# Token tiles of the latent q and kv projections on single banks of a PSUM pair

## The chip, the cores and the metric

One core of one Trainium2 chip runs one launch of the whole program. The metric is the device time of that launch in microseconds (us); lower is better. Runs of one kernel are given as the median with the lowest and the highest.

## What is computed

The reference is one inference step of a two-layer decoder for a prompt of 512 tokens and 8 samples of 4 tokens, 544 tokens in all, in float32. The change lies in the first layer's mixer, where multi-head latent attention and an S5 state-space layer stand side by side:

```
def even_mixer(hn, pos, h0_re, h0_im, attend, p):
    proj = hn @ p['w_in']                        # 1024 -> 768 (c_q), 256 (c_kv), 32 (k_r), 512 (u)
    cq = rms_norm(c_q, p['cq_norm'])
    qf = rms_norm((cq @ p['w_uq']).reshape(b, L, MLA_HEADS, MLA_QK), p['q_gain'])
    q = jnp.concatenate([qf[..., :MLA_NOPE], rope(qf[..., MLA_NOPE:], pos)], axis=-1)
    ckv = rms_norm(c_kv, p['ckv_norm'])
    kr = rope(k_r[:, :, None, :], pos)[:, :, 0]
    o_att = attend(q, ckv, kr)                   # keys and values: ckv @ w_ukv
    o_s5, hr, hi = s5_ssm(u, h0_re, h0_im, p)
    out = jnp.concatenate([o_att, o_s5], axis=-1) @ p['w_out']
```

After it come attention over a paged cache, cross-attention to a memory, a squared-ReLU MLP, and a second layer with a gated recurrence. None of that is edited.

## The kernel before

Every float32 matmul is made of three passes over a high and a low part (`mm3`, line 190 is where it issues them): high by high, high by low, low by high.

The first layer's mixer is `even_mixer`. It works in this order of the source: the S5 input `u` (four gemms), the S5 layer in four tiles of eight groups (`s5_layer`), the latent q `cq` (six gemms, line 394 and on), the latent kv `ckv` (loop at line 404), transposes of the kv latents (`plT`, `plTs`), the q heads (loop over two halves of the heads `ch` and five token tiles, lines 464 to 492), and the keys and values `kv` (loop at line 500). The token tiles run in the order 4, 0, 1, 2, 3; tile 4 holds the 32 sample tokens, the others 128 prompt tokens each. A q tile is 18 matmuls (6 blocks of the contraction by 3 passes) of 384 columns, a ckv tile 24 matmuls of 288 columns.

Each tile of S5 is a chain of its own: 16 small DMAs gather the input (`s5U`, line 872, on SP's queue) once the tile before has been read for the last time by its output matmuls; then the matmuls `s5X` (line 898), a scan on VectorE (lines 902 to 915) and the output matmuls `s5Y` (line 942).

The order of instructions on each engine is not written out by hand. A scheduler orders them when the program is built, by a timeline of its own: of what is ready it takes what stands first in the source. On the chip each engine then runs its list strictly in order. Weight loads are given higher priority (`load_w`): they go by SP's queue into a raw buffer (two of them), are split into a high part by ScalarE (line 165) and a low part by VectorE (line 166), in three buffers each. The q weights of one `ch` are three such pieces of two blocks each.

PSUM has eight banks. In this stage `pbig` hands out two tiles of two banks each (tag `big`, two buffers), three more banks are `small` and one is `side`. The q and ckv loops ask for a pair per token tile and use only its first bank:

```
            for t in (4, 0, 1, 2, 3):
                rows = rows_of(t)
                ps = self.pbig(f"q{t}_{ch}")[:, 0, :]
                self.tokmm(ps, (cH, cL), t, wq, 6, 0, 384)
```

A pair can be handed out again when everything that reads it is done. For a q tile that is: squares with sums on ScalarE (line 476), an addition on VectorE (477), a power on GpSimd (478), and four scaled copies on ScalarE (480), the last reader. For a ckv tile it is the scaled write of `lat` on VectorE (414), after the squares (410), an addition (412) and a power (413).

The last q matmul frees the buffers that the kv stage writes: the split `cT` takes the memory of `cH` and `cL`, and the kv weights take that of the q weights. The decode stage's page loads (line 1025, on SP's queue) wait for the last kv matmul.

Of the kernel before, what the change touches and what calls it, by code (L numbers as in the profile page):

```python
# [87 lines left out]
def rows_of(t):  # L88
    return 128 if t < 4 else NSAMP
# [15 lines left out]
class K:  # L105
# [28 lines left out]

    def pbig(self, name):
        return self.ps.tile([128, 2, 512], F32, tag="big", bufs=2, name=name)

    def psm(self, name):
        return self.ps.tile([128, 512], F32, tag="small", bufs=self.nsmall, name=name)
# [177 lines left out]
    def even_mixer(self, gs, beside):  # L317
# [83 lines left out]
        nc.gpsimd.memset(kr[:, 4], 0.0)  # L401
        ssr = IN.tile([128, TT], F32, name="ssr")
        ws = self.load_wk(w, KT, QL, CL + ROPE, "ckv")
        for t in (4, 0, 1, 2, 3):
            rows = rows_of(t)
            ps = self.pbig(f"ckv{t}")[:, 0, :]
            self.tokmm(ps, (H, L), t, ws, KT, 0, CL + ROPE)
            j = self.tp.tile([128, CL], F32, tag="junk", bufs=1, name="junk")
            ssc = self.tp.tile([128, 1], F32, tag="ssc", name="ssc")
            nc.scalar.activation(j[:rows], ps[:rows, :CL], AF.Square, accum_out=ssc[:rows])  # L410
            nc.scalar.activation(kr[:rows, t], ps[:rows, CL:CL + ROPE], AF.Copy, scale=r0[:rows, t:t + 1])
            nc.vector.tensor_scalar(ssc[:rows], ssc[:rows], 1.0 / CL, eq[:rows, t:t + 1], op0=ALU.mult, op1=ALU.add)
            nc.gpsimd.tensor_tensor(out=ssc[:rows], in0=ssc[:rows], in1=self.nhalf[:rows, :1], op=ALU.pow)
            nc.vector.scalar_tensor_tensor(out=self.lat[:rows, t, :CL], in0=ps[:rows, :CL], scalar=ssc[:rows],
                                           in1=gckv[:rows], op0=ALU.mult, op1=ALU.mult)
# [44 lines left out]
        for rows, t in ((128, slice(0, 4)), (NSAMP, slice(4, 5))):  # L460
            nc.vector.scalar_tensor_tensor(out=mq[:rows, t], in0=pst[:rows, t], scalar=QK * EPS / QL, in1=eq[:rows, t],
                                           op0=ALU.mult, op1=ALU.add)
        q_s = k_tok[:NSAMP, 3]
        for ch in range(2):
            wq = self.load_wk(a["w_mla_uq"][0], 6, 384 * ch, 384, f"uq{ch}")
            hs = slice(4 * ch, 4 * ch + 4)
            for t in (4, 0, 1, 2, 3):
                rows = rows_of(t)
                ps = self.pbig(f"q{t}_{ch}")[:, 0, :]
                self.tokmm(ps, (cH, cL), t, wq, 6, 0, 384)  # L470
                q = (q_tok[:, t, hs] if t < 4 else q_s[:, hs])
                p3 = ps[:rows, :384].rearrange("p (h d) -> p h d", h=4)
                sq = self.tp.tile([128, 4, QK], F32, tag="junk", bufs=1, name="qsq")
                ssq = self.tp.tile([128, 4], F32, tag="ssk", name="ssq")
                for i in range(4):
                    nc.scalar.activation(sq[:rows, i], p3[:, i], AF.Square, accum_out=ssq[:rows, i:i + 1])
                nc.vector.tensor_scalar(ssq[:rows], ssq[:rows], mq[:rows, t:t + 1], None, op0=ALU.add)
                nc.gpsimd.tensor_tensor(out=ssq[:rows], in0=ssq[:rows], in1=self.nhalf[:rows, :4], op=ALU.pow)
                for i in range(4):
                    nc.scalar.activation(q[:, i], p3[:, i], AF.Copy, scale=ssq[:rows, i:i + 1])  # L480
                if ch == 0:
                    continue
                q = q_tok[:, t] if t < 4 else q_s
                tmp = self.tp.tile([128, HEADS, ROPE], F32, tag="qrt", bufs=1, name="qrt")
                b = lambda x: x[:rows, t, None, :].to_broadcast([rows, HEADS, x.shape[2]])
                nc.vector.tensor_tensor(out=tmp[:rows, :, :16], in0=q[:, :, NOPE + 16:], in1=b(sin[:, :, :16]),
                                        op=ALU.mult)
                nc.vector.tensor_tensor(out=tmp[:rows, :, 16:], in0=q[:, :, NOPE:NOPE + 16], in1=b(sin[:, :, 16:]),
                                        op=ALU.mult)
                nc.vector.tensor_tensor(out=q[:, :, NOPE:], in0=q[:, :, NOPE:], in1=b(cos), op=ALU.mult)  # L490
                nc.vector.tensor_tensor(out=q[:, :, NOPE:], in0=q[:, :, NOPE:], in1=tmp[:rows], op=ALU.add)
# [7 lines left out]
        for t in (4, 0, 1, 2, 3):  # L499
# [5 lines left out]
            for hf in range(2):  # L505
                ps = pb[:, hf, :]
# [1487 lines left out]
```

## Time and profile before

| | us |
|---|---|
| median of 3 runs (lowest, highest) | 1981.86 (1979.16, 1982.23) |
| the profiled execution | 1982.57 |
| its span, first to last instruction | 1980.8 |
| TensorE busy | 1917.3 (97% of the span) |
| VectorE busy | 1163.0 (59%) |
| ScalarE busy | 804.2 (41%) |
| GpSimd busy | 472.2 (24%) |
| mean granted TensorE clock | 0.986 of full speed |

The profile page has six parts: busy time of each engine, the span in slices, the DMA queues, the chain of work that ended last, the costliest groups of instructions, and the DMA issues. PE is TensorE, PEld its weight loads, DVE is VectorE, ACT is ScalarE, POOL is GpSimd, and SP's queue issues most DMAs. A busy PE is not PE at its peak, since matmuls overlap. The page is an average of stages that differ; the stage in question lies between about 100 and 250 us, so the views of that stretch matter here.

### The profile page before, as it was taken

To read this page: it belongs to the slowest core of one execution; us is meant where nothing else is said; L and a number is where in the kernel's file an instruction comes from. 1 tells how busy PE (TensorE), PEld (TensorE's weight loads), DVE (VectorE), ACT (ScalarE), POOL (GpSimd) and SP (SyncE) were. 2 spreads that over 40 slices of the span, in tenths; PEclk is the share of its full clock that TensorE was granted. 3 is DMA by queue.
4 is the path that set the end of the run, shared out by engine and by line. 5 is a ranking of instruction groups with operands and counts; after the bars stand their busy time and mean duration, and the time that the engine had idled before them with its cause. 6 is when DMAs were issued, how large, how long until landed. Compare 5 with 4: busy or idle time off the path is not lost.

```text
span 1980.8 us, 39933 instructions
## 1 busy us (share of the span) xinstructions
PE 1917.3 (97%) x16089; PEld 1808.6 (91%) x16089; DVE 1163.0 (59%) x2264; ACT 804.2 (41%) x1546; POOL 472.2 (24%) x375
## 2 busy tenths in 40 slices
PE   8888899999999999999999999999999999999998
PEld 7777688889998979999999999999999799999998
DVE  7766566766765557433333568898865563434344
ACT  4455455545554444322222334444444432313131
POOL 4545245656552205000000110111132130000000
PEclk9888999999999999999999999999999999999999
DMA  6221231231334453322322332323325233223222
GB/s 150 71 57 36 59 79 49 54 85 52 93 101 108 145 169 100 96 86 87 95 86 86 91 100 85 101 81 97 91 66 173 85 102 90 86 86 96 86 86 78
DMA packets 317163, 179.42 MB, mean 91 GB/s; under 512 B 52242, under 2 KB 305267, under 8 KB 316979
## 3 DMA queue, kind: packets, MB, share of 16 engines
q1 hardware_dynamic: 289154, 164.47, 28.6%
q10 hardware_dynamic: 26224, 8.06, 1.7%
q0 software_dynamic: 1600, 4.34, 0.8%
q8 instruction: 127, 2.08, 0.4%
q14 instruction: 58, 0.47, 0.1%
HBM read 165.90 MB, written 9.82 MB: 89 GB/s over the span
## 4 chain that ended last, share of the span: by engine, by line
PE 87%; DVE 5%; ACT 2%; issue 2%; SPq 1%; DMA 1%; POOL 1%; ACTq 0%; POOLq 0%; DVEq 0%
PE ps_dn L190 19%; PE ps_up L190 19%; PE kp L1150 9%; PE ps_wo L190 5%; PE ps_hq L190 3%; PE ps_hi L190 3%; PE ps_hf L190 3%; PE ps_hg L190 2%; PE ps_mq L190 2%; PE ps_wmo L190 2%; PE mkv L190 2%; PE s5Y L942 1%; PE ct L289 1%; SPq L1025 1%; PE hatt L1754 1%
## 5 line engine op out<-in xcount | busy, mean ns | idle before, releaser
L190 PE MATMUL ps_dn<-hidH,wH_dn 128*128 128x272 f32 x1024 | 211.4, 287 | 0.0
L190 PE MATMUL ps_dn<-hidH,wL_dn 128*128 128x272 f32 x1024 | 211.2, 288 | 0.0
L190 PE MATMUL ps_up<-actH_f,wH_up 128*128 128x272 f32 x1024 | 211.2, 287 | 0.0
L190 PE MATMUL ps_dn<-hidL,wH_dn 128*128 128x272 f32 x1024 | 210.7, 287 | 0.0
L190 PE MATMUL ps_up<-actH_f,wL_up 128*128 128x272 f32 x1024 | 210.5, 288 | 0.0
L190 PE MATMUL ps_up<-actL_f,wH_up 128*128 128x272 f32 x1024 | 210.4, 287 | 0.0
L1160 POOL TENSOR_TENSOR ss<-ss,nhalf 128x32 f32<-128x32 f32 x32 | 173.7, 5429 | 95.4 <-DVE ss L1158 92.0
L1265 DVE TENSOR_TENSOR h<-ps_dn,h 128x544 f32<-128x544 f32 x64 | 46.4, 725 | 207.2 <-PE ps_dn L190 207.2
L190 PEld LDWEIGHTS ps_dn<-hidL,wH_dn 128*128 128x128 f32 x1024 | 160.2, 188 | 0.0
L190 PEld LDWEIGHTS ps_up<-actL_f,wH_up 128*128 128x128 f32 x1024 | 160.0, 188 | 0.0
L190 PEld LDWEIGHTS ps_dn<-hidH,wL_dn 128*128 128x128 f32 x1024 | 159.6, 189 | 0.1
L190 PEld LDWEIGHTS ps_dn<-hidH,wH_dn 128*128 128x128 f32 x1024 | 159.5, 188 | 0.0
L190 PEld LDWEIGHTS ps_up<-actH_f,wL_up 128*128 128x128 f32 x1024 | 159.4, 188 | 0.0
L190 PEld LDWEIGHTS ps_up<-actH_f,wH_up 128*128 128x128 f32 x1024 | 159.4, 188 | 0.0
L165 ACT ACTIVATE wH_dn<-wraw_dn 128x1024 fp32r<-128x1024 f32 x64 | 68.0, 1063 | 216.6 <-PE ps_dn L190 154.9
L165 ACT ACTIVATE wH_up<-wraw_up 128x1024 fp32r<-128x1024 f32 x64 | 68.0, 1062 | 195.4 <-PE ps_up L190 99.6
L166 DVE TENSOR_TENSOR wL_up<-wraw_up,wH_up 128x1024 fp32r<-128x1024 f32 x64 | 82.8, 1294 | 109.2 <-ACT wH_up L165 107.1
L166 DVE TENSOR_TENSOR wL_dn<-wraw_dn,wH_dn 128x1024 fp32r<-128x1024 f32 x64 | 78.4, 1224 | 67.5 <-ACT wH_dn L165 65.3
L1153 ACT ACTIVATE sq<-kp 128x512 f32<-128x512 f32 x128 | 76.4, 597 | 95.1 <-PE kp L1150 56.9
L253 POOL TENSOR_TENSOR acc_x<-acc_x,sq 128x544 f32<-128x544 f32 x7 | 10.8, 1544 | 349.6 <-issue 327.3
L1155 DVE TENSOR_REDUCE ss<-sq 128x8 f32<-128x512 f32 x128 | 86.8, 678 | 0.0
L165 ACT ACTIVATE hidH<-mu 128x544 fp32r<-128x544 f32 x64 | 42.2, 659 | 100.6 <-DVE mu L1576 100.6
(738 smaller groups left out, 5097.9 us busy)
## 6 DMA issues: line engine op xcount, KB each, us to landing
wraw_up<-in_w_mlp_up_dram SPq DMA_DIRECT2D x64, 512.0 KB, 4.1
wraw_dn<-in_w_mlp_down_dram SPq DMA_DIRECT2D x64, 512.0 KB, 3.6
cnat<-in_cache_mla_latent_dram SPq DMA_DIRECT2D x128, 128.0 KB, 2.2
mkc<-in_cache_mem_k_dram SPq DMA_DIRECT2D x16, 512.0 KB, 6.3
wraw_w_mem_k<-in_w_mem_k_dram SPq DMA_DIRECT2D x8, 512.0 KB, 4.5
wraw_w_mem_v<-in_w_mem_v_dram SPq DMA_DIRECT2D x8, 512.0 KB, 3.6
wraw_wo<-in_w_out_even_dram SPq DMA_DIRECT2D x8, 512.0 KB, 4.3
wraw_mq<-in_w_mem_q_dram SPq DMA_DIRECT2D x8, 512.0 KB, 3.6
```

Of the source, the lines that this page charges most:

```text
L165: i = nc.scalar.activation(H, x, AF.Copy)
L166: sub.tensor_tensor(out=L, in0=x, in1=H.bitcast(F32), op=ALU.subtract)
L190: nc.tensor.matmul(out, x, sl(y), start=first and n == 0, stop=last and n == 2)
L289: self.nc.tensor.transpose(out, in_, self.ident[:p, :p])
L942: nc.tensor.matmul(out, lhs, rhs, start=(n == 0), stop=(n == 4), skip_group_check=True, tile_position=(0, 32 * q))
L1025: load = lambda x, t, src: nc.sync.dma_start(x, src[bass.ds(pg[t], 1), 0].rearrange("o t c -> (o t) c"))
L1150: mm = nc.tensor.matmul(ps[:, hf, :272], x[:, t % 2, kt], wb[hf][y][:, kt], start=(kt == 0 and n == 0), stop=(kt == 1 and n == 2))
L1153: nc.scalar.activation(sq, ps[:, :, :256], AF.Square)
L1155: V.tensor_reduce(out=ss[:, t, :], in_=sq.rearrange("p f (h d) -> p (f h) d", h=4), op=A, axis=AX.X)
L1160: G.tensor_tensor(out=sf, in0=sf, in1=self.nhalf, op=ALU.pow)
L1265: self.nc.vector.tensor_tensor(out=halves(self.h[:, i, :]), in0=ps, in1=halves(self.h[:, i, :]), op=ALU.add)
L1754: nc.tensor.matmul(ps[64 * x:64 * x + 64, c * 96:(c + 1) * 96], kF[:, k0_:k0_ + 64], xt[:, x0:x0 + 96], start=True, stop=True, tile_positi ...
```

## The change

A generator is added that asks for a pair and hands out its first bank, then its second, and then asks for the next pair. Both loops take their bank from it: one generator for the ckv loop, and one for the q loop that runs on over both halves of the heads. The matmuls, their readers and the number of PSUM buffers stay as they are.

```diff
+    def half_banks(self, name):
+
+        while True:
+            t = self.pbig(name)
+            yield t[:, 0, :]
+            yield t[:, 1, :]
@@ the ckv loop
+        banks = self.half_banks("ckv")
         for t in (4, 0, 1, 2, 3):
             rows = rows_of(t)
-            ps = self.pbig(f"ckv{t}")[:, 0, :]
+            ps = next(banks)
@@ the q loop
+        banks = self.half_banks("q")
         for ch in range(2):
...
             for t in (4, 0, 1, 2, 3):
                 rows = rows_of(t)
-                ps = self.pbig(f"q{t}_{ch}")[:, 0, :]
+                ps = next(banks)
```

The ckv tiles now take three pairs: (4, 0), (1, 2), (3). The q tiles take five: (4, 0), (1, 2), (3 and tile 4 of the second half), (0, 1), (2, 3). A pair comes free when both of its tiles have been read.

## Rows read from the trace of the kernel before

**Rows 1.** The page's first part: busy us (share of the span) and instructions.
```profile
PE 1917.3 (97%) x16089; PEld 1808.6 (91%) x16089; DVE 1163.0 (59%) x2264; ACT 804.2 (41%) x1546; POOL 472.2 (24%) x375
```
**Rows 2.** The chain that ended last, 98 to 262 us: start, duration, what.
```profile
127.84 4.40 PE s5Y L942 x128
...
161.51 6.95 PE s5Y L942 x128
...
172.85 1.71 DMA s5U<-uT
...
198.47 4.98 PE s5Y L942 x135
...
227.36 5.88 PE kv L190 x24
233.26 0.36 SPq L1025
...
248.62 1.78 DMA cnat<-in_cache_mla_latent_dram
```
**Rows 3.** Timeline of PE, 98 to 216 us: start, duration, what [idle before <-releaser].
```profile
111.39 0.40 PE L190 MATMUL ckv<-wH_ckv,xgH 128*128 128x288 f32 x1 [0.59 <-ACT sq L252]
...
132.55 0.38 PE L190 MATMUL ckv<-wH_ckv,xgL 128*128 128x288 f32 x1
...
143.72 0.53 PE L190 MATMUL q<-wH_uq,cqH 128*32 128x384 f32 x1 [0.99 <-ACT k_tok L149]
...
148.25 0.63 PE L898 MATMUL s5X<-s5U,s5W 128*128 128x136 f32 x4
...
157.38 0.68 PE L942 MATMUL s5Y<-s5Hp,s5W 128*32 128x136 f32 x16 [0.84 <-DVE s5Hp L913]
159.93 0.71 PE L942 MATMUL s5Y<-s5Hp,s5W 128*32 128x136 f32 x16 [1.86 <-DVE s5Hp L913]
161.51 1.08 PE L942 MATMUL s5Y<-s5g,s5W 128*32 128x127 f32 x16 [0.88 <-DVE s5g L915]
...
183.17 0.44 PE L190 MATMUL q<-wH_uq,cqH 128*128 128x384 f32 x1 [2.58 <-ACT q_tok L480]
...
191.78 0.45 PE L190 MATMUL q<-wH_uq,cqH 128*128 128x384 f32 x1 [2.15 <-ACT k_tok L480]
...
194.86 0.34 PE L190 MATMUL q<-wH_uq,cqL 128*128 128x384 f32 x1
...
207.13 0.34 PE L190 MATMUL q<-wH_uq,cqL 128*128 128x384 f32 x1
...
211.95 0.63 PE L190 MATMUL kv<-wH_ukv,cTH 128*32 128x512 f32 x1 [1.69 <-ACT qTs L555]
```
**Rows 4.** Timeline of ACT, 100 to 250 us, same columns.
```profile
134.74 0.37 ACT L410 ACTIVATE junk<-ckv 128x256 f32<-128x256 f32 x1
...
143.07 0.60 ACT L149 ACTIVATE k_tok<-plT 128x512 f32<-128x512 f32 x1
...
161.17 0.57 ACT L480 ACTIVATE q_tok<-q,ssq 128x96 f32<-128x96 f32 x2
...
182.08 1.04 ACT L480 ACTIVATE q_tok<-q,ssq 128x96 f32<-128x96 f32 x4
```
**Rows 5.** Timeline of SP's queue, 104 to 216 us: start, time over all its issues, what.
```profile
132.26 10.92 SPq L872 DMA_DIRECT2D s5U<-uT  x16
...
168.48 10.02 SPq L872 DMA_DIRECT2D s5U<-uT  x16
178.61 0.52 SPq L178 DMA_DIRECT2D wraw_uq<-in_w_mla_uq_dram  x1
```
**Rows 6.** Timeline of DVE, 100 to 250 us, columns as in rows 3.
```profile
183.88 0.96 DVE L166 TENSOR_TENSOR wL_uq<-wraw_uq,wH_uq 128x768 fp32r<-128x768 f32 x1
```
**Rows 7.** Busy time by stretch: us, PE, PEld, DVE, ACT, POOL, granted clock, DMA share, GB/s.
```profile
160.00:164.00 4.00, 3.12 (x56) 1.96 (x60) 1.79 (x4) 2.65 (x9) 3.84 (x8) 0.56 0.02 4
...
175.00:212.00 37.00, 28.62 (x309) 23.78 (x308) 26.78 (x57) 24.23 (x101) 13.99 (x20) 0.95 0.24 70
```

## Prediction

> **What bounds the kernel now.** I read the page's first part, then the chain of work that ended last, then the timelines of the stretch from 100 to 250 us. Over the whole launch TensorE is busy 97% of the span [rows 1], but that is an average: nearly all the idle time that this change can touch lies in the first layer's mixer. The chain says why that stretch counts: the last keys-and-values matmul ends at 233.24, SP's first page load goes out at 233.26, the page loads take until 248.62, and the last of them lands 1.78 us later, where the decode stage begins [rows 2]. So whatever moves the last kv matmul earlier moves everything behind it, until another chain ends later. The kv stage in turn starts at 211.95, 4.5 us after the last q matmul (207.13 + 0.34 = 207.47) [rows 3], because its operands are written into the memory of the q stage's. I call that last q matmul E; it is the number to predict.
>
> In the PE timeline [rows 3] the reader is to see where PE stands still for a PSUM pair before E. A ckv tile waits 0.59 us for the last reader of the gemm before. Before 161.51 PE idles 0.84, 1.86 and 0.88 us for VectorE's scan, with no q matmul to fill in: the third q tile (t = 1) is done, and the next needs the pair that ScalarE releases at 161.17 + 0.57 = 161.74 [rows 4]. At 183.17 it waits 2.58 us for a pair, released at 182.08 + 1.04 = 183.12 [rows 4], and at 191.78 another 2.15.
>
> **The change, part by part.** A tile now waits for the readers of the tile three or four before it, where it waited for those two before. No wait is added in any engine's data flow, no instruction is added, no DMA moves past another by the edit itself. All of the effect is in when matmuls may start, and in the order that the scheduler then builds.
>
> *The ckv loop.* The 0.59 goes. More may hang on it: the last of ckv's 120 matmuls stands alone at 132.55, behind a whole block of s5Y [rows 3], and its readers start only at 134.74 [rows 4]; from there the transposes and the copy at 143.07 hold back the first q matmul at 143.72 [rows 3, 4]. A little more time in hand would put it ahead of that block, and then its readers' chain of 143.72 - 134.74 = 9.0 us runs beside s5Y. So q starts between 0 (the order stays) and 9 us earlier. What is late next is the gather of the third S5 tile: its 16 issues end at 132.26 + 10.92 = 143.18 and the last lands some 1.7 us later, about 144.9 [rows 2, 5], while s5X starts at 148.25, behind q's first tile [rows 3]. So an earlier q start is worth at most 148.25 - 144.9 = 3.35 us to the S5 chain. I take 1.5, nearly the middle, as the order is unknown.
>
> *The first half of the q heads.* The tile t = 2 can now run in the 3.58 us of idle before 161.51. A q tile's 18 matmuls start between 191.78 and 194.86 [rows 3], 3.08 / 17 = 0.18 us apart, 3.3 us in all, so it fits. s5Y itself starts no earlier, since VectorE's scan sets it. But it ran slow: the granted clock between 160 and 164 was 0.56 of full speed [rows 7], near the lower level of 1.2 GHz, after the idle. The block took 6.95 us, where the tile before took 4.40 [rows 2]. With matmuls in the gap I take 2.4 us off its end; the bounds are 0 and 6.95 - 4.40 = 2.55.
>
> *What this frees.* The gather of the last S5 tile starts when s5Y ends, at 168.48, occupies SP for 10.02 us, and only then does the last piece of the second half's q weights go out, at 178.61 [rows 5]; its low part is ready at 183.88 + 0.96 = 184.84 [rows 6]. All five tiles of the second half need it. With 2.4 + 1.5 it is ready at about 181. This is the wait that comes next: more banks can't pass it, they only let more tiles wait there with four of their six blocks done.
>
> *The second half.* At 184.84 the kernel before had done some 20 of the 90 matmuls: 12 of its first tile, and some 8 since 183.17 [rows 3]. With three tiles admitted (the third pair's second bank and both of the fourth) 36 can be done. That leaves 54 by 0.18 = 9.7 us. To it come one release of the third pair, for which the fourth tile must wait: at least the four scaled copies, 1.04 us, at most about the 9.0 of ckv's readers [rows 3, 4], and nearer the former, since other tiles' matmuls lie beside it; I take 2. And the last S5 tile's s5Y, 4.98 us [rows 2], takes precedence when it is ready and then lies before some of the q matmuls: 0 to 4.98, I take 4, as s5Y lay before E here too. E is then 181 + 9.7 + 2 + 4 = 196.7, against 207.47: 10.8 us earlier. The two waits of 2.58 and 2.15 are in that difference and are not counted again.
>
> *What is given back.* Between 175 and 212 VectorE is busy 26.78 us of 37 and ScalarE 24.23 [rows 7]. The same work in 26 us leaves VectorE no room; some of it moves ahead of 175, but queueing must grow. I give back 3 us. The kv stage (211.95 to 233.24, 21.3 us [rows 2, 3]) is bounded by its own readers and keeps its length; the glu gemm behind it and the page loads move with it.
>
> The sum: 10.8 - 3, some 8 us off. Against the profiled execution's own 1982.57 (its span 1980.8 and 1.8 around it) that is 1974.6; that execution lies 0.7 above the median 1981.86, so I forecast 1974 as a median.
>
> **The rivals.**
>
> *The stalls move, and nothing is won.* For it speaks that the last weights hang on s5Y, the scan and the gather, none of which the edit touches: if the clock does not recover and the order of ckv stays, the weights are ready at 184.84 as before, and if then s5Y lies ahead of the last two tiles and VectorE's queue gives back the rest, E moves by 16 matmuls' worth, 16 by 0.18 = 2.9 us, or less. That gives 1979 to 1982. Against it speaks that 4.7 us of idle (2.58 and 2.15) stood behind a bank and no weight.
>
> The Trainium skill ("TensorE: Matmul & The Clock Gate", the section "HAM oscillation — how this bites in real kernels") tells of a kernel with its contraction blocks back to back that gained next to nothing from a second PSUM buffer. By that rule this rival would hold; the trace speaks against it with the 2.58 and 2.15 us that PE stood before a bank.
>
> *Slower: the wrong work first.* The scheduler orders by its own timeline. With more banks it may put one or two whole q tiles (3.3 us each) ahead of s5X in PE's list where on the chip s5X is ready first. In the trace one such tile already stands there: s5X at 148.25, ready at 144.9 [rows 2, 3, 5]. If two more stand ahead for each of the two last S5 tiles, the S5 chain loses 2 by 6.6 = 13 us, less the 4.7 of waits removed: 8 us slower, 1990. It decides from where the added delay of s5X exceeds the removed waits, about one and a half tiles in all. Against it: s5X stands first in the source and wins whenever the builder's timeline sees it ready.
>
> *More than forecast.* If ckv's last matmul goes ahead of s5Y, the S5 chain starts the full 3.35 us earlier and s5Y of the last tile lies behind E, E comes to about 190 and the time to 1966.
>
> *The change doesn't do what it says.* If the second bank of a pair were held until the first is read, the tiles would go as before or worse; then 1982. Both banks are disjoint, and kv's two halves already use a pair's two banks side by side, so this is unlikely.
>
> **How the numbers follow.** Forecast (5 to 12 us off) 0.50; more than that 0.13; the stalls move 0.22; slower 0.10; not as it says 0.05. The forecast's own range is 1970 to 1977. The range for 8 in 10 reaches on to the better case's near edge and through the case of no gain: 1965 to 1982.5. A measurement of this kernel can tell about 0.2%, 4 us, from no change. Faster by more than that (below 1977.9): 0.50 and 0.13 and a little of the third case, 0.65. Within it: 0.25. Slower: 0.10.
>
> **What would show it.** Right: in the changed PE timeline no wait for `q_tok` or `k_tok` of line 480 before the tiles t = 0 and t = 1 of the second half; q matmuls in the gap before the third S5 tile's s5Y, and that block nearer 4.4 us than 6.95; PE waiting for the last weight piece instead, at about 181; the last q matmul near 197, the last kv matmul near 225, the first page load right behind it. The stages behind keep their lengths. Wrong: E as before with idle of the same size put down to VectorE, the gather or the weights (the second case); s5X later after its gather than 3.35 us (the slower case); or E earlier and the end not, which would mean that the chain through the kv stage is not the one that counts.

## The result and the profile after

The changed kernel takes 1999.81 us (median of five runs, 1994.49 to 2002.81), the kernel before, on the same chip, 1979.16 (1977.42 to 1982.23): the ratio is 1.0097, 95% interval 1.0084 to 1.0111. It is some 19 us slower, where 8 us faster was forecast. The profiled execution of after is the fastest of its five (span 1992.7, time 1994.49).

Executions of kernels whose PE lists are the same up to the ckv loop differ by up to 6 us when it begins (101.4 to 107.6), so I measure the stage from inside: from the end of the last `cq` matmul (106.87 in before, 101.54 in after) to the end of the last transpose `wkT`, behind the kv loop and the glu gemm (249.24 and 262.29). That is 142.4 us in before and 160.8 in after, 18.4 more. So the whole loss is in this stage.

The timeline of PE in after answers to [rows 3] (start, duration, what, [idle before <-releaser]; the lines of the code have moved by seven to nine: 422 is the write of `lat`, 489 the scaled copies of q, 487 the power on GpSimd):

```profile
106.05 0.40 PE L197 MATMUL ckv<-wH_ckv,xgH 128*128 128x288 f32 x1 [0.58 <-ACT sq L259]
...
116.16 0.37 PE L197 MATMUL ckv<-wH_ckv,xgH 128*128 128x288 f32 x1 [2.01 <-DVE lat L422]
...
171.33 0.44 PE L197 MATMUL q<-wH_uq,cqH 128*128 128x384 f32 x1 [1.40 <-ACT q_tok L489]
...
187.44 1.13 PE L951 MATMUL s5Y<-s5Hp,s5W 128*32 128x136 f32 x16 [6.79 <-POOL ssq L487]
...
205.83 0.44 PE L197 MATMUL q<-wH_uq,cqH 128*128 128x384 f32 x1 [3.29 <-ACT k_tok L489]
...
217.66 0.84 PE L296 MATMUL qks<-ident,k_tok 32*96 32x32 f32 x8 [3.69 <-ACT q_tok L489]
218.71 0.69 PE L197 MATMUL q<-wH_uq,cqH 128*128 128x384 f32 x1 [0.20 <-ACT q_tok L489]
...
224.23 0.34 PE L197 MATMUL q<-wH_uq,cqL 128*128 128x384 f32 x1
```

The waits for readers did not go, they grew. There is one in the ckv loop that before didn't have (2.01 us for `lat`, the last reader of a ckv tile), and behind the last S5 tile PE stands before `k_tok` and `q_tok` again, 3.29 us ahead of a q tile and 3.69 us ahead of the transposes `qks`, which take a pair as well. The longest wait, 6.79 us, the profile puts down to the power of a q tile; but `s5Hp`, which these matmuls read, was itself finished by VectorE only at 187.29. Before waits for the scan in the same place too, with one q tile to fill the time [rows 3]; here the next q tile stands behind the wait in PE's list. The last q matmul ends at 224.23 + 0.34 = 224.57.

The chain that ended last, after's answer to [rows 2] (start, duration, what):

```profile
156.44 7.18 PE s5Y L951 x128
...
188.58 5.55 PE q L197 x18
194.12 4.79 PE s5Y L951 x144
...
205.83 8.16 PE q L197 x36
...
217.62 1.04 ACT q_tok L489 x4
218.71 5.69 PE q L197 x17
...
226.91 6.86 PE kv L197 x22
```

Measured from the same point, the S5 chain has hardly moved: its last output matmuls end 97.3 us after the last `cq` matmul (198.88 - 101.54), in before 96.6 (203.43 - 106.87). What is late is q work that stands behind it: in before 22 matmuls, in after 72, which take from 198.88 to 224.57. The busy time by stretch (us; PE, PEld, DVE, ACT, POOL; granted clock, DMA share, GB/s) answers to [rows 7]:

```profile
160.00:164.00 4.00, 4.00 (x81) 3.17 (x78) 0.00 (x0) 1.02 (x2) 0.33 (x2) 0.67 0.01 4
175.00:212.00 37.00, 26.38 (x259) 22.76 (x258) 19.28 (x41) 16.82 (x69) 11.78 (x17) 0.82 0.19 54
...
218.70:224.00 5.30, 5.29 (x17) 5.29 (x18) 3.35 (x8) 2.42 (x3) 0.00 (x0) 0.50 0.00 0
```

Between 175 and 212 PE, VectorE and ScalarE all have less to do than in before; they wait for each other. The granted clock in it is 0.82 where it was 0.95: after the waits TensorE runs part of the time at the lower of its levels, 1.2 GHz (0.50 of full speed between 218.7 and 224.0), and the last q tile takes 5.86 us (218.71 to 224.57) where 3.3 are usual [rows 3].

Why the tiles wait is read from PE's instruction list. With a tile's number, and a stroke for the second half of the heads, the order in which PE takes them is (ckv first, then q by its place to the last two blocks of `s5Y`):

```
         ckv        ahead of the third | ahead of the last      | behind it
before   4 0 1 2 3  4 0 1              | 2 3 4' 0' 1' most of 2'| rest of 2', 3'
after    4 1 0 3 2  4 1                | 0 3 2 0'               | 4' 2' 1' 3'
```

Tiles 4 and 0 share a pair, then 1 and 2, and so on. Tile 1 is taken before tile 0: the second bank of a pair is not free while the first is in use. In the list the first matmul into a second bank carries a wait for VectorE (ckv) or ScalarE (q), the engine that reads the first bank last, unless PE has already waited for that reader. The builder orders writers and readers by the tile that was handed out, and that is the pair. A pair also comes free late: the ckv tile that waits 2.01 us is tile 3, fourth in the list, whose pair is that of tiles 4 and 0, and tile 0 ran just ahead of it.

### The profile page after: what moved, and what is told of

The parts are those of the page before. It is cut to its first block, busy times and chain, and to the rows that moved or that the text cites. A ratio compares the mean times of both kernels' runs of the same rounds, so it can differ in the third digit from the quotient of the medians.

```text
span 1992.7 us, 39927 instructions
## 1 busy us (share of the span) xinstructions
PE 1917.2 (96%) x16089; PEld 1810.8 (91%) x16089; DVE 1164.9 (58%) x2264; ACT 803.2 (40%) x1546; POOL 471.7 (24%) x375
## 4 chain that ended last, share of the span: by engine, by line
PE 85%; DVE 5%; SPq 2%; ACT 2%; DMA 2%; issue 2%; POOL 2%; POOLq 0%; DVEq 0%; ACTq 0%
PE ps_dn L197 19%; PE ps_up L197 19%; PE kp L1159 7%; PE ps_wo L197 5%; PE ps_hq L197 3%; PE ps_hi L197 3%; PE ps_hf L197 3%; PE ps_wmo L197 2%; PE ps_hg L197 2%; PE ps_mq L197 2%; PE mkv L197 2%; SPq L1034 1%; PE q L197 1%; PE s5Y L951 1%; PE ct L296 1%
## 5 line engine op out<-in xcount | busy, mean ns | idle before, releaser
L260 POOL TENSOR_TENSOR acc_x<-acc_x,sq 128x544 f32<-128x544 f32 x7 | 10.8, 1542 | 349.7 <-issue 327.3
```

What stands on the lines that cost most here:

```text
L260: nc.gpsimd.tensor_tensor(out=acc, in0=acc, in1=sq, op=ALU.add)
```

## The experiments

The table gives each run's ratio to before with its 95% interval, and from its profile the stage (last `cq` matmul to last `wkT`, before: 142.4), the end of the last q matmul and the start of kv, both counted from the first q matmul (before: 207.47 - 143.72 = 63.8, and 211.95 - 143.72 = 68.2 [rows 3]).

| run | what | ratio | stage | last q | kv |
|---|---|---|---|---|---|
| after | the change | 1.0097 (1.0084 to 1.0111) | 160.8 | 82.4 | 83.5 |
| e1_crossed | banks of two pairs taken crosswise | 0.9999 (0.9986 to 1.0012) | 142.3 | 63.8 | 68.2 |
| e2_four | four one-bank tiles, ckv and q | 1.0013 (1.0002 to 1.0024) | 143.5 | 51.6 | 66.1 |
| e3_ckv_only | the change in the ckv loop alone | 0.9997 (0.9987 to 1.0008) | 143.2 | 64.1 | 66.9 |
| e4_q_only | the change in the q loop alone | 1.0027 (1.0014 to 1.0040) | 146.7 | 71.8 | 72.9 |
| e5_four_q | four one-bank tiles, q alone | 0.9971 (0.9957 to 0.9985) | 137.1 | 49.6 | 63.2 |
| e6_pairs_q | two tiles fill a pair, then both are read | 0.9997 (0.9986 to 1.0008) | 143.5 | 60.8 | 69.2 |
| e7_before_nopow | before without q's power on GpSimd | 0.9985 (0.9976 to 0.9995) | 139.3 | 63.4 | 66.5 |
| e8_four_nopow | e2_four without it | 0.9990 (0.9978 to 1.0002) | 143.7 | 44.3 | 58.1 |
| e9_q_depth2 | e5_four_q with two tiles | 1.0018 (1.0007 to 1.0030) | 146.4 | 64.0 | 71.1 |
| e10_q_depth3 | e5_four_q with three | 0.9996 (0.9984 to 1.0008) | 141.6 | 59.4 | 66.5 |
| e11_q_four_pool | e5_four_q, kv's low parts on GpSimd | 0.9970 (0.9958 to 0.9982) | 136.8 | 49.5 | 63.1 |
| e12_before_pool | before, the same | 1.0009 (0.9994 to 1.0025) | 144.3 | 63.7 | 68.2 |
| e13_q_four_nopow | e5_four_q without the power | 0.9981 (0.9972 to 0.9990) | 137.6 | 51.0 | 62.2 |
| e14_q_four_nopow_pool | both | 0.9967 (0.9955 to 0.9979) | 135.6 | 48.9 | 60.4 |

With one exception (e8_four_nopow, 3 us) the change of the stage, taken from one profile, agrees within 2 us with that of all runs' time by the ratio. So the stage is what these edits act on.

### Is it the pair?

```
 def half_banks(self, name):
     while True:
-        t = self.pbig(name)
-        yield t[:, 0, :]
-        yield t[:, 1, :]
+        t, u = self.pbig(name + "a"), self.pbig(name + "b")
+        for b in range(2):
+            yield t[:, b, :]
+            yield u[:, b, :]
```

> Edit: the generator asks for two pairs at once and hands out first bank of the one, first bank of the other, then second bank of the one, second bank of the other. The number of banks is that of the change; only which tile shares a pair with which differs. Theory 1 (the second bank of a pair is held until the first bank's readers are done, so a pair is one place in the queue and not two): every tile then waits for the readers of the tile two before, as in the kernel before; the time is that of before, 1977 to 1983 us, last q matmul near 207, no q matmul waits for the tile just ahead of it. Theory 2 (the four banks are free of each other and the loss comes from more work in flight, which the builder's order puts in the wrong place): four tiles are in flight here too; the time stays near that of the change, 1994 to 2003 us.

Measured 0.9999. Both banks of both pairs are still used in turn; only which tiles share a pair has changed: neighbours in time no longer do. PE's instruction list is that of before again, tile for tile, and so are its waits:

```profile
140.32 0.53 PE L190 MATMUL qa<-wH_uq,cqH 128*32 128x384 f32 x1 [0.99 <-ACT k_tok L149]
...
179.77 0.45 PE L190 MATMUL qa<-wH_uq,cqH 128*128 128x384 f32 x1 [2.58 <-ACT q_tok L480]
...
188.39 0.44 PE L190 MATMUL qb<-wH_uq,cqH 128*128 128x384 f32 x1 [2.14 <-ACT k_tok L480]
...
203.74 0.34 PE L190 MATMUL qb<-wH_uq,cqL 128*128 128x384 f32 x1
...
208.54 0.64 PE L190 MATMUL kv<-wH_ukv,cTH 128*32 128x512 f32 x1 [1.68 <-ACT qTs L555]
```

The last q matmul ends 63.76 us after the first, in before 63.75. If the second bank were free at once, four tiles would be in flight here too; there are two. A pair is one place in the queue, whichever of its banks is written.

The two loops by themselves (the other one as in before):

> Edit: the change in the ckv loop alone; q as before. Theory 1: tile 0 is held behind tile 4's readers and tile 2 behind tile 1's, ckv ends some microseconds later against the S5 work, and with it the transposes and the start of q; 1 to 6 us slower than before, the smaller part of the loss. Theory 2: nothing measurable, as ckv has few tiles and little to reorder, 0 to 2 us.

> Edit: the change in the q loop alone; ckv as before. Theory 1: the larger part of the loss, 12 to 20 us slower than before: the tile in the second bank of each pair starts only after the reader chain of the first, and the third pair ties the last tile of the first half of the heads to the first tile of the second. Theory 2: all of the loss, 15 to 21 us.

The ckv loop alone has the wait of 2.01 us for `lat` and costs nothing that can be measured. The q loop alone costs 0.27%, about 5 us. Both expectations for e4_q_only (12 to 21 us) were too high, and so was the 1 to 6 us of the first for e3_ckv_only. Where the 5 us lie, the timeline of PE in e4_q_only shows:

```profile
184.39 0.36 PE L190 MATMUL q<-wH_uq,cqH 128*32 128x384 f32 x1 [2.26 <-ACT q_tok L480]
...
192.91 0.44 PE L190 MATMUL q<-wH_uq,cqH 128*128 128x384 f32 x1 [2.14 <-ACT k_tok L480]
...
209.89 0.84 PE L289 MATMUL qks<-ident,k_tok 32*96 32x32 f32 x8 [4.00 <-ACT q_tok L480]
210.87 0.69 PE L190 MATMUL q<-wH_uq,cqH 128*128 128x384 f32 x1
```

The last tile, 3', is the second bank of the pair of 2' and needs the readers of 2'. It stands in the list behind the transposes `qks`, which wait 4.00 us for the pair of 0' and 1'; no other work is left to fill the time, and kv follows it. Together the two loops cost 19 us and not 5. The lists say how: with its tiles out of order the ckv loop ends later (27.9 us after the last `cq` matmul in after, 26.1 in before), the first q matmul comes 40.6 us after it and not 36.9, and in the list only two q tiles stand ahead of the third block of `s5Y`, not three. In e4_q_only the tiles 4 1 0 stand ahead of it and only part of 1' and 3' behind the last block; in after four whole tiles do, two in flight, each behind readers. That the order does it is read from these lists; no run changes the order alone. The late start is not enough by itself: in e3_ckv_only the first q matmul comes even later (42.0 us after the last `cq` matmul), two q tiles stand ahead of the third block, the last `s5Y` ends 102.7 us after that point, 6 us later than in before, and still the stage is only 0.8 us longer. There a single q tile, 3', stands behind the last block:

```profile
145.24 0.68 PE L190 MATMUL q<-wH_uq,cqH 128*32 128x384 f32 x1
...
205.54 0.42 PE L942 MATMUL s5Y<-s5U,s5T 128*32 128x136 f32 x8
205.89 0.44 PE L190 MATMUL q<-wH_uq,cqH 128*128 128x384 f32 x1
```

So the loss goes with the q tiles left behind the last S5 block, each behind readers, and not with how late q or S5 is.

### What are four in flight worth?

```
-                ps = self.pbig(f"q{t}_{ch}")[:, 0, :]
+                ps = self.one(f"q{t}_{ch}")
+    def one(self, name):
+        return self.pb.tile([128, 512], F32, tag="one", bufs=4, name=name)
```

The four banks of the two pairs are handed out here as four tiles of one bank for the time of the loop, from a memory pool of their own; the pairs come back behind it.

> Edit: the four banks are handed out as four tiles of one bank each, from a PSUM pool of their own that is opened for the ckv loop, the transposes and the q loop and closed before kv; the gemms before and behind use pairs as before. Theory 1 (the pair held its second bank): now four tiles are truly in flight, the last q matmul moves to some 190 to 200 us and the time falls by 5 to 12 us against the kernel before, to 1967 to 1975 us, as the prediction's sum said of the change. Theory 2 (more in flight is what hurts): as slow as the change or slower, 1994 us and more.

> Four separate one-bank tiles as in the run e2_four, but for the q tiles (and qks) alone; the ckv tiles and the transposes take pairs as before, so that nothing is asked of the banks until the ckv loop is over. In e2_four the first ckv tile started some 3 us late behind the gemm that still held the banks. Theory A (the gain of four in flight is real, and e2_four lost it at the change of pools): 5 to 8 us faster than before, about 1973. Theory B (the readers of the q tiles, on ScalarE, VectorE and GpSimd, set the start of the kv loop, whenever the q matmuls end): within 2 us of before, with the last q matmul some 10 us earlier than before's 207.5 and the first kv matmul less than 4 us earlier than before's 211.95.

e2_four gains nothing (1.0013), and the 5 to 12 us expected of it did not come. Its first ckv matmul starts 5.3 us after the last `cq` matmul, which before's overlaps: ahead of it the list now has `s5X`, which waits 2.55 us for its gather, and ckv then waits 0.78 us for the last reader of the gemm, since the new pool must wait until the gemm has let go of the banks. Without the new pool there, e5_four_q is 0.29% faster, 5.7 us. Its timeline of PE (488 to 492 are now the lines of q's readers, 928 and 930 those of the last S5 tile's `s5Hp` and `s5g`):

```profile
142.71 0.53 PE L199 MATMUL q<-wH_uq,cqH 128*32 128x384 f32 x1
...
181.78 0.54 PE L199 MATMUL q<-wH_uq,cqH 128*32 128x384 f32 x2 [1.99 <-ACT wH_uq L174]
...
192.00 0.34 PE L199 MATMUL q<-wH_uq,cqL 128*128 128x384 f32 x1
...
196.63 1.13 PE L957 MATMUL s5Y<-s5Hp,s5W 128*32 128x136 f32 x16 [2.74 <-DVE s5Hp L928]
...
200.13 1.08 PE L957 MATMUL s5Y<-s5g,s5W 128*32 128x127 f32 x16 [2.36 <-DVE s5g L930]
...
205.90 0.41 PE L199 MATMUL kv<-wH_ukv,cTH 128*32 128x512 f32 x1
```

The last q matmul comes 49.6 us after the first, 14 us earlier than in before, but kv only 5 us earlier: 9 us are given back between the two. Where it is given back was the next question; first, whether the gain comes from the depth at all:

```
-        return self.pb.tile([128, 512], F32, tag="one", bufs=4, name=name)
+        return self.pb.tile([128, 512], F32, tag="one", bufs=2, name=name)
```

(and three in e10_q_depth3)

> The kernel of e5_four_q with two one-bank tiles in place of four: the same new pools and places, but two q tiles in flight as before. If the 4 us that e5_four_q gained come from the depth: within 2 us of before, the second half of the heads waiting again for q_tok's copies. If they come from the pools (kv's pair no longer behind qks and the last q tiles in one queue): as fast as e5_four_q, about 1975.

> The same with three one-bank tiles. Before's waits for readers in the second half of the heads were 2.58 and 2.15 us, and a q tile is 3.4 us of matmuls, so that one tile more covers them: as fast as e5_four_q within 2 us, if depth is what counts; the fourth bank then does nothing.

It does: 1.0018 with two tiles, 0.9996 with three, 0.9971 with four. With two, the waits of before are back in e9_q_depth2's timeline of PE, and the separate pool costs one of its own ahead of kv, whose pair now waits for the last q tile's readers:

```profile
181.81 0.44 PE L199 MATMUL q<-wH_uq,cqH 128*128 128x384 f32 x1 [2.56 <-ACT q_tok L492]
...
190.44 0.45 PE L199 MATMUL q<-wH_uq,cqH 128*128 128x384 f32 x1 [2.15 <-ACT k_tok L492]
...
213.31 0.64 PE L199 MATMUL kv<-wH_ukv,cTH 128*32 128x512 f32 x1 [4.40 <-ACT q_tok L492]
```

So in this arrangement the third and fourth tile together are worth 1.0018 - 0.9971 = 0.47%, 9 us; against before up to 3.6 us of that go to the pool (1.0018). My expectation for e10_q_depth3, that three would do, was wrong: the third gives half of it.

The other way to four in flight without a pool is to fill both banks of a pair before either is read:

```
+                if t in (4, 1, 3):
+                    p2 = self.pbig(f"q{t}_{ch}")
+                    for b, u in enumerate((4, 0) if t == 4 else (1, 2) if t == 1 else (3,)):
+                        pb[u] = p2[:, b, :]
+                        self.tokmm(pb[u], (cH, cL), u, wq, 6, 0, 384)
+                ps = pb[t]
```

> Four q tiles in flight in another way, with no new pool: the matmuls of two tiles fill both banks of a pair (tiles 4 and 0, 1 and 2, 3 alone, in each half of the heads) before anything is read from the pair. The second bank then never waits for readers of the first, as the kv loop does it with its two halves. Theory A (four in flight is worth what the prediction's sum said): 5 to 8 us faster. Theory B (the readers set the start of the kv loop): within 2 us of before; a reader may have to wait for the matmuls of both tiles of its pair, up to 3.4 us later than now for the first tile, so up to 3 us slower is possible.

No change (0.9997). The last q matmul comes 3 us earlier, but the last tiles' readers then come in one lot; in e6_pairs_q's timeline of PE nothing runs while they do:

```profile
208.03 0.84 PE L289 MATMUL qks<-ident,k_tok 32*96 32x32 f32 x8 [6.27 <-ACT q_tok L485]
209.74 0.64 PE L190 MATMUL kv<-wH_ukv,cTH 128*32 128x512 f32 x1 [0.87 <-ACT q_tok L485]
```

### What gives the gain back?

In e5_four_q's timeline of GpSimd one power of the q tiles stands out:

```profile
188.03 1.00 POOL L490 TENSOR_TENSOR ssq<-ssq,nhalf 128x4 f32<-128x4 f32 x1
...
193.92 7.28 POOL L490 TENSOR_TENSOR ssq<-ssq,nhalf 128x4 f32<-128x4 f32 x1 [3.01 <-DVE ssq L489]
...
201.34 1.01 POOL L490 TENSOR_TENSOR ssq<-ssq,nhalf 128x4 f32<-128x4 f32 x1
```

The same instruction, 1.0 us elsewhere, takes 7.28; in e2_four it is 7.28 too, at 196.76. ScalarE's copy of that tile waits 5.71 us for it, so it is no slip of the record. VectorE is busy without a gap all that time (timeline of DVE, e5_four_q), until 200.3, and the power ends 0.88 us after that, about its usual length:

```profile
194.77 1.21 DVE L175 TENSOR_TENSOR wL_ukv<-wraw_ukv,wH_ukv 128x1024 fp32r<-128x1024 f32 x1
195.90 0.67 DVE L928 TENSOR_TENSOR s5Hp<-s5g,s5w 128x512 f32<-128x512 f32 x1
...
196.84 1.21 DVE L175 TENSOR_TENSOR wL_ukv<-wraw_ukv,wH_ukv 128x1024 fp32r<-128x1024 f32 x1
...
198.11 1.27 DVE L175 TENSOR_TENSOR cTL<-k_tok,cTH 128x1088 fp32r<-128x1088 f32 x1
199.31 0.67 DVE L930 TENSOR_TENSOR s5g<-s5g,s5w 128x512 f32<-128x512 f32 x1
199.91 0.41 DVE L503 TENSOR_TENSOR q_tok<-q_tok,qrt 128x256 f32<-128x256 f32 x1
```

Two suspects, then, and both stand ahead of kv: the held power (and with it the last q tiles' readers), and VectorE's list, in which kv's weights lie before `s5Hp` and `s5g` of the last S5 tile (2.74 and 2.36 us of waits on PE). Taking the power away, in before and in e2_four (q is then scaled by a constant and not normalised):

```
-                nc.gpsimd.tensor_tensor(out=ssq[:rows], in0=ssq[:rows], in1=self.nhalf[:rows, :4], op=ALU.pow)
+                nc.vector.tensor_scalar(ssq[:rows], ssq[:rows], 0.0, 0.0625, op0=ALU.mult, op1=ALU.add)
```

> The kernel before with the GpSimd power of the q tiles (ssq, 10 instructions of 1.0 to 1.1 us) left out: a VectorE instruction writes a constant in its place, so q is not normalised; every wait and tile stays. It is the control for the next run. The readers of each tile get shorter by the power and a hop to GpSimd and back, about 1 us a tile. Theory B: the waits for banks in the second half of the heads (2.58 and 2.15 us) shorten by about 1 us each, 1 to 3 us faster than before. If the readers don't matter: within 1 us.

> The kernel of e2_four (four one-bank tiles) with the same GpSimd power left out, q not normalised. In e2_four's profile one of these powers, at 196.8, took 7.3 us where the others take 1.0, while VectorE ran without a gap until 203.2, and ScalarE waited 5.8 us for it; all q tiles' last readers and the kv loop stood behind it. Theory B1 (that held power ate the gain): the first kv matmul comes 5 to 7 us earlier than e2_four's, and the time is at least 4 us below e7_before_nopow. Theory B2 (VectorE's own work, which the earlier q tiles press together with the last S5 tile's, is the bound): within 2 us of e7_before_nopow.

Before gains 0.15%, 3 us, as the readers' turn gets shorter. e8_four_nopow decides less than was hoped: kv starts 8 us earlier than in e2_four (58.1 for 66.1), but the builder has also moved the last block of `s5Y` behind the first matmuls of kv, where it comes at 212.93 and holds them up; the time is within a few us of its control, 0.9990 against 0.9985. Taking VectorE's share away instead:

```
-ON_POOL = ("u2", "u3", "cq0")
+ON_POOL = ("u2", "u3", "cq0", "ukv0_0", "ukv1_0")
```

> The kernel of e5_four_q with the low parts of the two kv weights (1.21 us each on VectorE, standing in its list ahead of the last S5 tile's s5Hp and s5g) made on GpSimd instead, 2.4 to 2.5 us each by the same subtraction of wL_u. In e5_four_q the last S5 tile's output matmuls waited 2.74 us for s5Hp and 2.36 us for s5g, and the kv loop stood behind them. Theory B2 (VectorE's list there is what took most of the 14 us by which the last q matmul came earlier): s5Y ends 2 to 4 us earlier, kv starts 2 to 4 us earlier, and 2 to 4 us faster than e5_four_q. Theory B1 (the long power on GpSimd, which also stands ahead of kv): GpSimd gets 4.9 us more work, so no gain, or up to 4 us slower than e5_four_q.

> The control: the kernel before with the low parts of the two kv weights on GpSimd in the same way. In before these stand behind the last S5 tile's scan (VectorE makes them at 207.3 to 209.6, when s5Y has ended), and kv waits for qTs's and the cT parts: 2.47 us on GpSimd in place of 1.2 us on VectorE can only come later; 0 to 3 us slower than before.

In before the same edit changes nothing that can be told from noise (1.0009). In e11_q_four_pool the waits of `s5Y` fall from 2.74 and 2.36 us to 1.61 and 0.48, as the theory of VectorE's list had it, but kv starts no earlier (63.1 us after the first q matmul, in e5_four_q 63.2), and the time is that of e5_four_q. GpSimd, with the subtraction first in its list, was held itself (timelines of POOL and of DVE, e11_q_four_pool):

```profile
190.26 8.04 POOL L175 TENSOR_TENSOR wL_ukv<-wraw_ukv,wH_ukv 128x1024 fp32r<-128x1024 f32 x1 [1.31 <-ACT wH_ukv L174]
198.27 1.02 POOL L490 TENSOR_TENSOR ssq<-ssq,nhalf 128x4 f32<-128x4 f32 x1
199.26 2.37 POOL L175 TENSOR_TENSOR wL_ukv<-wraw_ukv,wH_ukv 128x1024 fp32r<-128x1024 f32 x1
```

```profile
194.82 1.27 DVE L175 TENSOR_TENSOR cTL<-k_tok,cTH 128x1088 fp32r<-128x1088 f32 x1
200.39 1.38 DVE L498 TENSOR_TENSOR qrt<-q_tok,ctab 128x128 f32<-128x128 f32 x1 [4.30 <-ACT q_tok L492]
```

The first subtraction takes 8.04 us and the second, with VectorE idle for the first half of it, 2.37; the first ends 2.2 us after VectorE fell idle (194.82 + 1.27 = 196.09). Like the held power it ends about its usual length after VectorE's last instruction, as if it had hardly advanced before; that is a reading of two cases. The Trainium skill ("Perfetto Trace Analysis", section "Optimizing Scalar/DVE Operations") says that GpSimd and VectorE share a read port of SBUF, so that moving work from one to the other may not help. The trace agrees: 8.04 against 2.37 us, and 0.9970 against 0.9971 for the time. That it is the port no run here shows.

Both suspects at once:

> The kernel of e5_four_q with GpSimd's power of the q tiles left out (a constant written by VectorE in its place, q not normalised). On TensorE the last S5 tile's output matmuls stay ahead of kv, and on VectorE its s5Hp now stand ahead of the kv weights. In e5_four_q the last q matmul came 49.6 us after the first, the first kv matmul 63.2 us after it (before: 63.75 and 68.2). If the held power (7.28 us) is what keeps kv from following: kv starts 56 to 60 us after the first q matmul and the time is 1967 to 1972, 3 us or more below e7_before_nopow (1975.9) and e5_four_q (1975.2). If ScalarE's and VectorE's own work at the end of the loop is the bound: kv starts 62 to 64 us after it, within 2 us of e5_four_q.

> The same, and the low parts of the two kv weights on GpSimd as in e11_q_four_pool. Now neither the power nor the weights stand ahead of the last S5 tile or of the last q tiles' copies, but the weights themselves may come late, since a subtraction on GpSimd took 8.0 us where it ran beside a busy VectorE. If VectorE's list is what is left: 1 to 3 us faster than e13_q_four_nopow. If GpSimd is held again: as fast or up to 3 us slower, kv waiting for wL_ukv.

With only the power taken away kv starts 62.2 us after the first q matmul, not 56 to 60: the held power is not the bound by itself, and the time (0.9981) is no better than e5_four_q's. `s5Y` still waits in e13_q_four_nopow's timeline of PE:

```profile
191.97 0.68 PE L957 MATMUL s5Y<-s5Hp,s5W 128*32 128x136 f32 x16 [1.54 <-DVE s5Hp L928]
...
195.86 1.08 PE L957 MATMUL s5Y<-s5g,s5W 128*32 128x127 f32 x16 [2.11 <-DVE s5g L930]
```

With both gone kv starts at 60.4, 2.8 us earlier than in e5_four_q, and the stage is 1.5 us shorter; of the 9 us given back between the last q matmul and kv 2 are regained (11.5 us between the two, 13.6 in e5_four_q, 4.5 in before), which in the total (0.9967 against 0.9971) is within the intervals. By the medians it is 2.4 us faster than e13_q_four_nopow, as expected if VectorE's list is what is left, but these intervals overlap too. Even then two of VectorE's instructions run long beside the subtractions on GpSimd, which take 7.60 us from 190.75 (timeline of DVE, e14_q_four_nopow_pool):

```profile
193.85 2.30 DVE L498 TENSOR_TENSOR qrt<-q_tok,ctab 128x128 f32<-128x128 f32 x1
196.07 2.42 DVE L500 TENSOR_TENSOR qrt<-q_tok,ctab 128x128 f32<-128x128 f32 x1
```

These two take 0.28 us each elsewhere. So neither suspect alone, nor both, takes the gain back. What is left is the joint work of VectorE and GpSimd between the last q matmuls and kv: the last S5 tile's scan, kv's weights, `cTL`, and the last tiles' powers and rotations, which the earlier matmuls push together. That this is the rest is read from the timelines and not shown: the remaining 7 us were not taken apart further.

## Why the prediction was wrong

*The chain was right.* The last kv matmul sets the page loads and they set the rest: in after kv ends at 246.32 and the first page load goes out at 246.34. But for e8_four_nopow every change of this stage came out in the time within 2 us.

*The failed step is the first of the change part: "A tile now waits for the readers of the tile three or four before it."* In the changed kernel every second tile waits for the readers of the tile right before it in the source, which shares its pair, and nothing is gained in depth: with the pairs taken crosswise (e1_crossed) the two tiles in flight, the waits of 2.58 and 2.14 us and the time (0.9999) are those of before. The case "the change doesn't do what it says" named just this, at 0.05. Its reason against was that the banks are disjoint and that kv uses both of a pair side by side. But kv writes both halves before anything reads either; the q and ckv loops would write one while the other is read, and of that the trace of before had no example. The instruction list of the changed kernel, or e1_crossed, was the evidence; the trace of before could not give it.

*The price of that case was wrong too.* I took 1982, "as before or worse". For the q loop alone it was 5 us worse, for both 19, because the tiles change their order in PE's list and four of them end up behind the last S5 tile with nothing beside them. "No wait is added" fell with it: 2.01 us in ckv, 4.00 at the end of e4_q_only's q loop.

*The sum, where its premise holds.* e5_four_q is what I priced, for q alone. The gap before the third `s5Y` block is filled but for 0.88 us, and the block runs from 160.69 to 165.28, 4.6 us, against my 6.95 - 2.4. PE next waits for the last weights, at 181.78 (I said about 181). The last q matmul comes 13.6 us earlier, counted from the last `cq` matmul; I had 10.8, of which 1.5 for an earlier start of q that no run showed. The term that was off is the one "given back": 3 us taken, 9.1 measured. I had put VectorE's 26.78 us of 37 [rows 7] as nearly full and still let 8 us through; its work and GpSimd's then lay in each other's way, which I had not priced. The net was 5.7 us instead of 8, or 9 against the same arrangement with two tiles; that it lies nearer than its two terms is luck in part, since they missed in opposite directions.

*The ckv part was wrong.* The 0.59 stayed (0.58), q started 3.7 us later and not 0 to 9 us earlier, and with four one-bank tiles ckv started 5.3 us late at the change of pools and then took no less time (27.7 us against 26.2 in before).

*The rival "nothing is won"* does not hold for this loop where more tiles really are in flight: from two tiles to four the ratio goes from 1.0018 to 0.9971. The kernel cited for it (the Trainium skill, "TensorE: Matmul & The Clock Gate", section "HAM oscillation — how this bites in real kernels") gained next to nothing from a second PSUM buffer. No run here goes from one buffer to two, so this neither confirms nor refutes it.

*The slower case* had the right sign with another mechanism: in after 12 of the 16 `s5X` matmuls of the third S5 tile run from 137.4 to 142.5, ahead of the first q tile, and the last four at 147.45; no further q tile went ahead of them.

## What to carry to other kernels

Count what is in flight by what the program hands out and takes back, not by banks: two halves of one buffer are one place as soon as one half is written while the other is read, and the order of instructions may get worse than without them. Ask of such a split which existing code both writes and reads the halves alternately; a loop that fills both first is no example. And when an engine's work is to end earlier, price what then runs together behind it, engine by engine, and GpSimd and VectorE together.

## What was not expected of the hardware

An instruction on GpSimd can take many times its usual time while VectorE is busy without a gap: a power of 128x4 took 7.28 us in two kernels (e2_four, e5_four_q) and 3.27 in a third (e10_q_depth3), else 1.0 to 1.7; a subtraction of 128x1024 took 8.04 in e11_q_four_pool, where those of the first gemms take 2.4 to 2.6. Both long ones ended about their usual length after VectorE's run of instructions was over (0.88 and 2.2 us). It goes the other way too: VectorE's 0.28 us took 1.38 (e11_q_four_pool), 2.30 and 2.42 (e14_q_four_nopow_pool) beside GpSimd's subtraction. Not every busy stretch does it: in before a power ran in 1.12 us at 192.26 beside VectorE's scans. Which of VectorE's instructions hold GpSimd was not tried.

The fastest kernel here that computes the whole reference is e11_q_four_pool (1972.95 us, ratio 0.9970), level with e5_four_q (0.9971): four one-bank tiles for the q loop alone.
